# Two layers of a hybrid backbone on one core: the mixer in another order, attention's projections through DRAM, one attention routine

## The chip, the cores and the metric

The kernel runs on one core of a Trainium2 chip. The metric is the device time of one execution in microseconds. TensorE is called PE here (its weight loads, which overlap it, PEld), VectorE is DVE, ScalarE is ACT, GpSimd is POOL; SP is the queue that issues the DMAs.

## The reference, cut to what matters

Input is a latent stream x of 512 tokens and a context of 256 tokens, each 1024 wide. There are two layers. A layer is a feed-forward (half step), a mixer, and another feed-forward (half step):

```python
h, hc = modulate(rms_norm(x, g1), ..), modulate(rms_norm(xc, g1), ..)
p = h @ w_in[l]; pc = hc @ w_in[l]              # 3456 columns, cut into the groups' inputs
out_a = window_attn(rope(qa), rope(ka), va, ctx keys, sink)     # 4 heads of 64, window 128
out_b = global_attn(rope(norm(qb)), all keys, all values)       # 4 heads
out_c = retention, forward and backward, * silu(gates)          # 4 heads, chunks of 128
out_d = RWKV-7 recurrence, forward and backward, * (sigmoid(gd) @ g2)
x  = x  + mod[5]   * concat(out_a, out_b, out_c, out_d) @ w_out[l]
xc = xc + mod_c[5] * (the same for the context)                 # layer 0 only
```

The context sees only itself, and its mixer output is needed in layer 0 alone. So in layer 1 the queries, the gates and the outputs are made for 512 tokens, the keys and values for 768.

## The kernel before, in words

Activations lie transposed: a tile holds 128 features on the partitions and the tokens along the free dimension. The stream is eight such tiles, xT (128x768), which stay in SBUF through the whole program. Large products with a weight (feed-forward and `proj`, L926) run in three fp32r passes: weight and activation are each split in a high and a low part (`split`, L371: ACT makes the high part, DVE the rest), and `mm3` (L361) adds high*high, high*low, low*high. The split activations hh and hlo are made by the last step of the feed-forward. All other products are plain fp32, and each of those appears in the trace as two MATMULs.

`proj` loads one block of 128 columns of w_in (1024x128, 512 KB), splits it, runs 24 steps of `mm3` into two PSUM banks, and DVE (L945) and ACT (L946) bring the result to SBUF. A layer has 27 such blocks: ten for retention (C), eight for the attentions (A and B: k, v and two q tiles each) and nine for the recurrence (p0 to p8). A projection for all 768 tokens is called wide here, one for 512 tokens (layer 1's queries, gates, p0, p1, p6) half.

`mixer` (L1283) emits, in this order:

1. `group_c` twice: ten projections and retention.
2. `proj_ab` twice: eight projections, rotary, head norms, values turned to tokens on partitions.
3. `attend` (L1003): attention A, one unit for each head and block of 128 queries. A unit is scores (64 rows of the PE) into one PSUM tile of two banks (pool pS, one buffer), maximum (DVE), exp (ACT), a pass on DVE that divides by the sum, transposes, copies, and the product with V.
4. The nine projections p7, p8, p2, p3, p4, p5, p0, p1, p6; after p8 `rw_low`, after p3 `rw_lengths`.
5. The recurrence `rw_scan` (L844) over six blocks of 128 tokens in stages: decay (d), operands (o), inverse (i), late (l), steps (s), norm and output (y). All of attention B (`attend2`) is emitted between the first decay and the first operands. B's keys are padded with zeros to 128 rows, and its P*V takes two query blocks at a time; division by the sum comes at the end.
6. `out_proj` with A and C (64 fp32 products in layer 0), as a filler, then `out_proj` with B and D.

The Tile framework orders each engine's instructions when the program is built: emission order is the priority, and what is emitted later fills an engine when what is earlier isn't ready by the framework's own estimate. So step 3 runs among the projections of step 4, and step 6's first half among the steps of the recurrence. On the chip each engine takes its instructions in that fixed order and waits on semaphores. SP issues all DMAs, also in one fixed order.

The only state from one block of the recurrence to the next is S in `rw_step` (L770). `rw_inverse` (L705) is a chain of 30 small DVE operations (L725, L727) between transposes, ACT copies and four PE round trips; its start can be read from the one large transpose into Bu (L716), one for each block.

Of the kernel before, what the change touches and what calls it, by code (L numbers as in the profile page):

```python
# [113 lines left out]
class Whole:  # L114
    def __init__(self, ctx, tc, aps):
        self.tc, self.nc, self.a = tc, tc.nc, aps
        self.banks = {}
        self.macc = None
        self.const = self.pool(ctx, "const", 1)
        self.xp = self.pool(ctx, "xp", 1)  # L120
        self.work = self.pool(ctx, "work", 2)

    def psum(self, name, tag):
        pool, n = self.banks[tag]
        return pool.tile([128, 512], F32, name=name, tag=tag, bufs=n)

    def setup(self):
# [5 lines left out]
        self.xT = [self.xp.tile([128, T], F32, name=f"xT{k}") for k in range(KT)]  # L133
# [154 lines left out]
    def halves(self):  # L288
        t = self.pS.tile([128, 2, 512], F32, name="rst", tag="S")
        return [t[:, 0, :], t[:, 1, :]]  # L290

# [43 lines left out]
    def ready(self, l, n):  # L335

        def cb(k):
# [3 lines left out]
            self.raw_tile(k)  # L341
        return cb

# [116 lines left out]
    def rw_cols(self, l):  # L460
# [43 lines left out]
        self.rw2 = self.mp.tile([128, 2, 256], F32, name=f"rw2{l}")  # L504
# [29 lines left out]
    def rw_open(self, ctx):  # L534
        self.rp = self.pool(ctx, "rp", 1)
# [19 lines left out]
    def rw_lengths(self, p):  # L555
# [3 lines left out]
        for j in range(2):  # L559
            for d in range(2):  # L560
                z = self.ring("zkk")
# [282 lines left out]
    def rw_scan(self, p, bon, ctx_out, first):  # L844

        S = None
        N = T // 128
        has_r = lambda u: u > 1 or ctx_out
        st = [None] * (N + 2)
        Y = None  # L850

        def stage(k, u):
            nonlocal S, Y
# [11 lines left out]
            if k == "s":  # L865
                Y = self.rt.tile([128, NCH, 128], F32, name="Y", tag="Y", bufs=1) if h else None
                for c in range(NCH // 2):
                    S = self.rw_step(st[u], c, S, Y, h, u == 0 and c == 0)
            if k == "y" and h:
                self.rw_norm(Y)  # L870
                self.rw_out(Y, u, bon)

        stage("d", 0)
        for _ in first:
            pass
        for k, u in (("o", 0), ("d", 1), ("i", 0), ("l", 0)):
            stage(k, u)
        for u in range(N):
            for k, i in (("o", 1), ("s", 0), ("i", 1), ("d", 2), ("l", 1), ("y", 0)):
                stage(k, u + i)  # L880
# [43 lines left out]
    def proj(self, l, cols, both, evac):  # L924

        nc = self.nc  # L926
        r = self.praw.tile([128, KT, 128], F32, name="pw", tag="pw")
        o = 0
        for c0, n in cols:
# [587 lines left out]
```

## Time and profile before

| | |
|---|---|
| median of 3 runs | 3537.83 us (3533.33 to 3539.41) |
| the profiled execution | 3531.58 us, of it span 3529.8 us |
| granted PE clock, mean | 0.982 |
| busy of the span | PE 96%, PEld 78%, DVE 57%, ACT 32%, POOL 5% |
| chain that ended last | PE 84%, DVE 10%, ACT 3% |
| HBM read, written | 260.68 MB, 2.10 MB |

A busy PE is not PE at its peak: a matmul's record runs from its start to the end of its pipeline, so records overlap, and the distance of two starts in a dense row is what a matmul takes. The mixer of layer 0 lies at about 634 to 1340 us of the span, that of layer 1 at 2512 to 3112 us.

### The profile page before, as it was taken

The numbers are of one execution on the slowest core, as the hardware profiler recorded it, in microseconds if no ns is written. First come the engines' busy times: TensorE is split into PE (matmuls) and PEld (weight loads), VectorE is DVE, ScalarE is ACT, GpSimd is POOL, SyncE is SP. The second block draws the span as 40 slices with busy tenths as digits, with TensorE's granted clock in tenths as the row PEclk, the third lists the DMA queues.
The fourth block names the chain that finished last, engine by engine and source line by source line (L and its number), as shares of the span: only waits on it lengthen the run. The fifth ranks groups of instructions, "written<-read, shape, count | busy, mean of one in ns | idle before, by whom it ended". The sixth has DMA issues, their size and how long they took to land.

```text
span 3529.8 us, 54945 instructions
## 1 busy us (share of the span) xinstructions
PE 3372.1 (96%) x22756; PEld 2738.7 (78%) x22756; DVE 2002.2 (57%) x4351; ACT 1145.6 (32%) x2173; POOL 166.6 (5%) x350
## 2 busy tenths in 40 slices
PE   6999999999988899999999999999999988989997
PEld 5888888878666667888888788888878766557776
DVE  5776664555567856654335765543556577653333
ACT  3211122323456633121213221221324477432222
POOL 0000000000022400000000000000000023100000
PEclk9999999999999999999999999999999989999999
DMA  7444331211100014332222443330211100143230
GB/s 235 126 133 130 108 115 40 59 37 49 31 6 2 8 36 141 114 99 79 62 60 66 126 132 120 91 109 27 75 43 50 35 1 5 28 124 102 89 103 24
DMA packets 324122, 266.33 MB, mean 75 GB/s; under 512 B 27396, under 2 KB 273312, under 8 KB 323872
## 3 DMA queue, kind: packets, MB, share of 16 engines
q1 hardware_dynamic: 323872, 262.82, 24.4%
q8 instruction: 179, 2.93, 0.3%
q14 instruction: 71, 0.58, 0.1%
HBM read 260.68 MB, written 2.10 MB: 74 GB/s over the span
## 4 chain that ended last, share of the span: by engine, by line
PE 84%; DVE 10%; ACT 3%; DMA 1%; issue 1%; POOL 1%; SPq 0%; DVEq 0%; ACTq 0%; POOLq 0%
PE ul L365 13%; PE ul L369 13%; PE ul L367 13%; PE y L369 6%; PE y L367 6%; PE y L365 6%; PE pj L365 4%; PE pj L367 4%; PE pj L369 4%; PE op L1276 3%; PE S L1018 1%; PE ch L782 1%; DVE xtmp L725 1%; DVE w1l L378 1%; PE po L1018 1%
## 5 line engine op out<-in xcount | busy, mean ns | idle before, releaser
L365 PE MATMUL ul<-hh,w1h 128*128 128x512 f32 (+1 forms) x2464 | 693.5, 350 | 6.4 <-ACT w1h L377 5.6
L367 PE MATMUL ul<-hl,w1h 128*128 128x512 f32 (+1 forms) x2464 | 693.1, 348 | 0.0
L369 PE MATMUL ul<-hh,w1l 128*128 128x512 f32 (+1 forms) x2464 | 688.8, 348 | 2.2 <-DVE w1l L378 2.2
L365 PEld LDWEIGHTS ul<-hh,w1h 128*128 128x128 f32 x2464 | 395.9, 190 | 80.3 <-issue 9.9
L367 PEld LDWEIGHTS ul<-hl,w1h 128*128 128x128 f32 x2464 | 396.9, 190 | 64.1 <-issue 0.8
L369 PEld LDWEIGHTS ul<-hh,w1l 128*128 128x128 f32 x2464 | 393.7, 189 | 65.3 <-DVE w1l L378 3.7
L367 PE MATMUL y<-gl,w2h 128*128 128x512 f32 x1232 | 343.0, 347 | 4.3 <-DVE gl L431 4.0
L369 PE MATMUL y<-gh,w2l 128*128 128x512 f32 x1232 | 339.4, 346 | 5.8 <-DVE w2l L378 5.8
L365 PE MATMUL y<-gh,w2h 128*128 128x512 f32 (+1 forms) x1232 | 340.2, 347 | 1.1 <-ACT gh L430 0.9
L377 ACT ACTIVATE w1h<-w1r 128x2048 fp32r<-128x2048 f32 x88 | 168.7, 1917 | 479.6 <-PE ul L367 451.6
L215 DVE SCALAR_TENSOR_TENSOR macc<-wm,sc,macc 128x512 f32<-128x512 f32 x392 | 274.7, 749 | 78.8 <-DMA wm<-in_w_mod_dram 77.5
L445 DVE SCALAR_TENSOR_TENSOR xT<-y,gate,xT 128x512 f32<-128x512 f32 x336 | 199.3, 633 | 192.7 <-PE y L369 192.3
L377 ACT ACTIVATE w2h<-wo 128x512 fp32r<-128x512 f32 (+1 forms) x192 | 111.5, 594 | 547.0 <-PE y L367 351.8
L365 PE MATMUL pj<-hh,pwh 128*128 128x512 f32 (+2 forms) x864 | 251.8, 343 | 3.9 <-DVE qA L945 1.8
L369 PE MATMUL pj<-hh,pwl 128*128 128x512 f32 (+2 forms) x864 | 243.1, 336 | 2.4 <-DVE pwl L378 2.4
L367 PE MATMUL pj<-hl,pwh 128*128 128x512 f32 (+2 forms) x864 | 244.0, 337 | 0.0
L419 DVE TENSOR_TENSOR u<-ul,rsb 128x512 f32<-128x512 f32 (+1 forms) x132 | 70.9, 553 | 302.5 <-PE ul L369 302.5
L369 PEld LDWEIGHTS y<-gh,w2l 128*128 128x128 f32 x1232 | 195.0, 188 | 39.8 <-DVE w2l L378 10.0
L367 PEld LDWEIGHTS y<-gl,w2h 128*128 128x128 f32 x1232 | 195.4, 188 | 38.2 <-DVE gl L431 8.8
L365 PEld LDWEIGHTS y<-gh,w2h 128*128 128x128 f32 x1232 | 195.7, 188 | 37.6 <-ACT w2h L377 3.1
L378 DVE TENSOR_TENSOR w1l<-w1r,w1h 128x2048 fp32r<-128x2048 f32 x88 | 201.4, 2289 | 28.3 <-ACT w1h L377 28.3
L421 ACT ACTIVATE sg<-sg,ub 128x512 f32<-128x512 f32 (+1 forms) x132 | 74.2, 609 | 424.4 <-DVE ub L416 319.9
(355 smaller groups left out, 4495.9 us busy)
## 6 DMA issues: line engine op xcount, KB each, us to landing
w1r<-in_ffn_w_in_dram SPq DMA_DIRECT2D x176, 512.0 KB
wm<-in_w_mod_dram SPq DMA_DIRECT2D x72, 1024.0 KB
wo<-in_ffn_w_out_dram SPq DMA_DIRECT2D x88, 512.0 KB
pw<-in_w_in_dram SPq DMA_DIRECT2D x46, 512.0 KB
pw<-in_w_in_dram SPq DMA_DIRECT2D x16, 256.0 KB
wo<-in_w_out_dram SPq DMA_DIRECT2D x128, 32.0 KB
wo<-in_w_out_dram SPq DMA_DIRECT2D x64, 64.0 KB
xl<-in_x_dram SPq DMA_DIRECT2D x4, 512.0 KB
```

The costliest lines, as they stand in the source:

```text
L215: nc.vector.scalar_tensor_tensor(out=acc[v], in0=r[:, k, :], scalar=s, in1=acc[v], op0=ALU.mult, op1=ALU.add)
L365: nc.tensor.matmul(p, lhsT=wh, rhs=xh[:, o:o + n], start=first, stop=False)
L367: nc.tensor.matmul(p, lhsT=wh, rhs=xl[:, o:o + n], start=False, stop=False)
L369: nc.tensor.matmul(p, lhsT=wl, rhs=xh[:, o:o + n], start=False, stop=last)
L377: nc.scalar.activation(out=hi, in_=raw, func=AF.Copy)
L378: nc.vector.tensor_tensor(out=lo, in0=raw, in1=hi, op=ALU.subtract)
L419: nc.vector.tensor_tensor(out=dst[:, o:o + n], in0=p, in1=self.rsb[:, o:o + n], op=ALU.mult)
L421: nc.scalar.activation(out=dst[:, o:o + n], in_=dst[:, o:o + n], func=AF.Silu, bias=b[:, u, s:s + 1])
L445: nc.vector.scalar_tensor_tensor(out=xs, in0=py[s], scalar=gt[s][:, n_:n_ + 1], in1=xs, op0=ALU.mult, op1=ALU.add)
L725: nc.vector.tensor_tensor(out=tmp[:, :, :, :n], in0=Xv[:, :, :, s:16], in1=Bv[:, :, s:16, s].unsqueeze(2).to_broadcast([128, 2, 4, n]), op ...
L1018: mm = lambda out, lt, r, st, sp: nc.tensor.matmul(out, lhsT=lt, rhs=r, start=st, stop=sp, skip_group_check=True)
L1276: nc.tensor.matmul(p, lhsT=w[i], rhs=os[i][:, osegs[i][v][0]:osegs[i][v][0] + c], start=i == 0, stop=i == m - 1)
```

## The change

Order of the new mixer: retention with its ten projections; p7, p8, p2, p3, then p0, p1, p4, p5; the recurrence, with p6 and the eight attention projections emitted behind all its stages; then a second phase with both attentions and both output projections.

- The pool of xT is closed when the mixer begins. `put_away` writes each finished tile to DRAM in the last step of the feed-forward, and the tiles are read back for the output projections. Retention's two results and the eight attention inputs go to DRAM (`leave`) and are read back (`fetch`) in the second phase.
- A projection loads and splits its weight in two halves of 256 KB. For p6 and the attention inputs the load, the split and the way out of PSUM have a raised priority, the matmuls have not.
- One routine `attend` serves A and B: scores on 64 rows for both, two score buffers of two banks each, one bank (`ptr`) for the transposes, one query block at a time, division by the sum at the end (as B before).
- hh and hlo stay allocated. Retention has banks of its own (ms 2, ra 2, ro 1).
- `out_proj` takes C and D first, then A and B.

```diff
     def mixer(self, l, last_cb):
...
+        self.xx.close()
+        self.pd = {}
...
+    def scan_phase(self, sx, l, ctx_out, segs, bon, bons):
...
+            for j in range(2):
+                self.group_c(l, j, ctx_out)
...
+            for i in (7, 8):
+                proj(i)
+            self.rw_low(p[7], p[8])
+            for i in (2, 3):
+                proj(i)
+            self.rw_lengths(p)
...
+        stage = self.rw_scan(p, bon, ctx_out)
+        stage("d", 0)
+        for i in (0, 1, 4, 5):
+            proj(i)
+        for k, u in (("o", 0), ("d", 1), ("i", 0), ("l", 0)):
+            stage(k, u)
+        for u in range(T // 128):
+            for k, i in (("o", 1), ("s", 0), ("i", 1), ("d", 2), ("l", 1), ("y", 0)):
+                stage(k, u + i)
+        proj(6, True)
+        for g in range(2):
+            for name, cols, both in self.cols_ab(g):
+                self.proj_away(l, name, cols, ctx_out or both)
+        self.rw_gate(l, p[6], segs)
+        for j in range(2):
+            self.rw_final(l, j, bons[j], p[6], segs)
...
+    def heads_phase(self, tx, l, ctx_out, segs, gate, bons, last_cb):
+        self.psum_open(tx, pj=2, ptr=1, po=1)
+        self.alias = {"ms": "pj"}
+        self.pS = self.pool(tx, "pS", 2, space=PSUM)
...
+            for g in range(2):
+                self.prep_ab(g, ctx_out, *ab[g])     # fetch, head norms, rotary, V
+            self.wop = self.pool(px, "wop", 3)
+            for g in range(2):
+                for _ in self.attend(g, *ab[g], ctx_out):
                     pass
+            self.xT = [self.x_tile(k, "xT") for k in range(KT)]
+            for j in range(2):
+                self.fetch(f"oc{j}", oc[j])
+            for k in range(KT):
+                nc.sync.dma_start(out=self.xT[k][:, :n1], in_=self.away[k])
...
+            self.out_proj(l, [[(512 + 128 * i, 128)] for i in range(4)], oc + bons, ...)
+            self.out_proj(l, rows(0) + rows(1), ab[0][1] + ab[1][1], ..., last_cb)
...
     def proj(self, l, cols, both, evac, soon=False):
+        near = self.tc.high_priority if soon else ExitStack
+        H = KT // 2
+        for h in range(2):
+            with near():
+                r = self.praw.tile([128, H, 128], F32, name="pw", tag="pw")
...
+                wh, wl = self.split(r, [128, H, 128], "pw", self.phl)
+            for k in range(H):
+                self.mm3(...)
+    def proj_away(self, l, name, cols, both):
+        s = self.stg.tile([128, 771], F32, name="stg", tag="stg", bufs=2)
+        self.proj(l, cols, both, self.to_tile(s), soon=True)
+        with self.tc.high_priority():
+            self.leave(l, name, s, T if both else SEQ)
```

## Rows read from the trace of the kernel before

**Rows 1.** Six stretches of the mixers: us, busy (count) of each engine, PEclk, DMA

```profile
634.00:857.00 223.00, 218.94 (x1323) 175.29 (x1322) 110.89 (x263) 64.13 (x103) 2.45 (x28) 1.00 0.20 53
857.00:1018.00 161.00, 158.11 (x934) 119.37 (x934) 88.16 (x274) 74.35 (x172) 6.25 (x11) 0.98 0.09 26
1018.00:1301.00 283.00, 249.82 (x3408) 179.15 (x3407) 213.87 (x685) 172.31 (x477) 80.05 (x143) 0.97 0.04 11
2512.00:2695.00 183.00, 179.51 (x1212) 151.39 (x1211) 97.03 (x245) 57.05 (x97) 2.48 (x28) 1.00 0.24 64
2695.00:2828.00 133.00, 131.63 (x858) 104.08 (x858) 76.78 (x232) 65.81 (x140) 5.26 (x10) 1.00 0.11 32
2828.00:3085.00 257.00, 225.52 (x3139) 160.39 (x3138) 190.72 (x600) 162.74 (x442) 67.06 (x120) 0.92 0.04 11
```

**Rows 2.** Timeline of PE, a wide projection, then a half one: start, us, what

```profile
658.53 0.51 PE L365 MATMUL pj<-hh,pwh 128*128 128x512 f32 x2
658.88 0.52 PE L367 MATMUL pj<-hl,pwh 128*128 128x512 f32 x2
...
2692.18 0.40 PE L365 MATMUL pj<-hh,pwh 128*128 128x256 f32 x2
2692.42 0.41 PE L367 MATMUL pj<-hl,pwh 128*128 128x256 f32 x2
```

**Rows 3.** Line L946, both mixers: duration min/median/max, first to last start

```profile
L946 ACT ACTIVATE p<-p,pb x18: 494/608/726, 871.0 to 1018.5; 128x512 f32<-128x512 f32 x9, 128x256 f32<-128x256 f32 x9
L946 ACT ACTIVATE p<-p,pb x18: 492/506/727, 2709.5 to 2828.4; 128x256 f32<-128x256 f32 x12, 128x512 f32<-128x512 f32 x6
```

**Rows 4.** Line L716, layer 0 and its last three blocks, layer 1 likewise

```profile
L716 DVE STREAM_TRANSPOSE Bu<-Bc x6: 1242/1245/1246, 1048.1 to 1241.5; 128x1024 f32<-128x1024 f32 x6
L716 DVE STREAM_TRANSPOSE Bu<-Bc x3: 1245/1245/1246, 1175.4 to 1241.5; 128x1024 f32<-128x1024 f32 x3
L716 DVE STREAM_TRANSPOSE Bu<-Bc x6: 1234/1245/1246, 2852.5 to 3039.8; 128x1024 f32<-128x1024 f32 x6
L716 DVE STREAM_TRANSPOSE Bu<-Bc x3: 1245/1245/1245, 2967.3 to 3039.8; 128x1024 f32<-128x1024 f32 x3
```

**Rows 5.** Exponentials of attention A, layer 0, layer 1: duration, first to last start

```profile
L1037 ACT ACTIVATE P<-S,st x24: 475/689/808, 881.9 to 984.1; 128x512 f32<-128x512 f32 x8, 128x640 f32<-128x640 f32 x8, 128x256 f32<-128x256 f32 x8
L1037 ACT ACTIVATE P<-S,st x16: 673/740/797, 2719.0 to 2794.5; 128x512 f32<-128x512 f32 x8, 128x640 f32<-128x640 f32 x8
```

**Rows 6.** Two groups in 857 to 1018: busy us, mean ns, idle before

```profile
L567 PE MATMUL kkss<-mean,zkk 128*128 128x2 f32 x48 | 5.7, 246 | 0.0
...
L378 DVE TENSOR_TENSOR pwl<-pw,pwh 128x1024 fp32r<-128x1024 f32 x8 | 9.8, 1219 | 0.0
```

**Rows 7.** Timeline, weight loads of one unit of attention A [idle before, releaser]

```profile
943.84 0.73 PEld L1018 LDWEIGHTS S<-kv,qA 64*128 64x128 f32 x4 [0.25 <-ACT st L1038]
945.11 0.42 PEld L1048 LDWEIGHTS ptr<-ident,P 128*128 128x128 f32 x4 [0.54 <-issue]
946.57 0.85 PEld L1018 LDWEIGHTS po<-PT,kv 128*64 128x64 f32 x14 [0.26 <-ACT PT L1049]
```

**Rows 8.** Timeline of PE, output projections of layer 0, end of layer 1's

```profile
1334.82 1.88 PE L1276 MATMUL op<-qB,wo 128*128 128x512 f32 x4
1336.54 1.88 PE L1276 MATMUL op<-kv,wo 128*128 128x512 f32 x4
...
3110.57 1.88 PE L1276 MATMUL op<-kv,wo 128*128 128x512 f32 x4
```

**Rows 9.** Timeline of PE, retention's scores of one head and of two

```profile
782.81 0.49 PE L1221 MATMUL ra<-q,k 64*128 64x128 f32 x2
...
784.17 0.49 PE L1221 MATMUL ra<-q,k 64*128 64x128 f32 x4
```

**Rows 10.** Two weight loads issued after layer 0's mixer, and the first matmul behind

```profile
1339.31 1.00 SPq L393 DMA_DIRECT2D w1r<-in_ffn_w_in_dram  x2
...
1347.33 1.01 PE L365 MATMUL ul<-hh,w1h 128*128 128x512 f32 x2 [1.49 <-ACT w1h L377]
```

More of the change, by code (lines that the diff above doesn't have):

```diff
@@ L865, in stage @@
             if k == "s":
-                Y = self.rt.tile([128, NCH, 128], F32, name="Y", tag="Y", bufs=1) if h else None
-                for c in range(NCH // 2):
-                    S = self.rw_step(st[u], c, S, Y, h, u == 0 and c == 0)
+                c[1] = self.rt.tile([128, NCH, 128], F32, name="Y", tag="Y", bufs=1) if h else None
+                for i in range(NCH // 2):
+                    c[0] = self.rw_step(st[u], i, c[0], c[1], h, u == 0 and i == 0)
             if k == "y" and h:
[L870 to L880, printed above, removed]
+                self.rw_norm(c[1])
+                self.rw_out(c[1], u, bon)
+        return stage
     def pool(self, ctx, name, bufs, **k):
@@ L922, in first_mods, with proj @@
             self.raw_shifts(0, 0)
-    def proj(self, l, cols, both, evac):
+    def proj(self, l, cols, both, evac, soon=False):
         nc = self.nc
-        r = self.praw.tile([128, KT, 128], F32, name="pw", tag="pw")
-        o = 0
-        for c0, n in cols:
-            nc.sync.dma_start(out=r[:, :, o:o + n], in_=self.a["w_in"][l, :, c0:c0 + n].rearrange("(k p) n -> p k n", p=128))
-            o += n
-        wh, wl = self.split(r, [128, KT, 128], "pw", self.phl)
+        near = self.tc.high_priority if soon else ExitStack
@@ new lines, in proj_away, with leave, fetch @@
+    def proj_away(self, l, name, cols, both):
[3 more added lines that the diff above has]
+            self.leave(l, name, s, T if both else SEQ)
+    def leave(self, l, name, s, n):
+        t = self.dram.tile([128, n], F32, name=f"{name}d{l}")
+        self.nc.sync.dma_start(out=t, in_=s[:, :n])
+        self.pd[name] = t, n
+    def fetch(self, name, t):
+        d, n = self.pd[name]
+        self.nc.sync.dma_start(out=t[:, :n], in_=d)
+        return t
@@ L1001, in tokens_major, with attend @@
             nc.scalar.copy(V[:, b0:b0 + nb, :], pt[:, :nb * 128].rearrange("p (b n) -> p b n", n=128))
-    def attend(self, ab, ctx_out):
-        nc = self.nc
-        kT, qs, V = ab[0][0], ab[1:3], ab[3].rearrange("p (b n) -> p b n", n=128)
+    def attend(self, g, kT, qs, V, ctx_out):
+        nc, ap = self.nc, self.ap
+        mm = lambda out, lt, r, st, sp: nc.tensor.matmul(out, lhsT=lt, rhs=r, start=st, stop=sp, skip_group_check=True)
+        hs = [(hf, slice(64 * hf, 64 * hf + 64)) for hf in range(2)]
@@ L1216, in group_c @@
                 hs = [(e, slice(64 * e, 64 * e + 64)) for e in range(2)]
-                pts = [self.psum("ra", tag) for tag in ("ptr", "ms")]
+                pts = [self.psum("ra", "ra") for e in range(2)]
                 for e, r in hs:
@@ L1236, in group_c @@
                                 nc.tensor.matmul(ws(r, d), lhsT=state[d][b][r], rhs=qw[d][r, cs], start=False, stop=True, skip_group_check=True)
-            for d in range(2):
-                nc.scalar.copy(od[d][:, o_:o_ + n], po[:, d, :n])
+                for d in range(2):
+                    nc.scalar.copy(od[d][:, cs], po[:, d * 128:(d + 1) * 128])
         for d in range(2):
@@ L1361, in rope_tab @@
-    def rope_tab(self, c0, r0):
+        self.xx.close()
+        self.pd = {}
+        with ExitStack() as mx:
+            self.bp = self.pool(mx, "bp", 1, side="right")
+            bon = self.bp.tile([128, 2, T], F32, name="bon")
+            bons = [bon[:, j, :] for j in range(2)]
+            with ExitStack() as sx:
+                self.scan_phase(sx, l, ctx_out, segs, bon, bons)
+            with ExitStack() as tx:
+                self.heads_phase(tx, l, ctx_out, segs, gate, bons, last_cb)
+            self.alias = {}
```

452 lines of the change are left out of this document (190 added, 262 removed).

## The prediction

> **What bounds the kernel now.** I read the busy shares first (the table above): PE is busy in 96% of the span, so only stretches where its work is thin have something to give. The busy time by stretch finds them, once each mixer is cut at places where the code changes over: the end of the first eighteen projections, of the last projection, of the recurrence with the first output projection [rows 1]. Up to 857 us (layer 0) PE is busy in 219 of 223 us. From 857 to 1018, nine projections with attention A between them, in 158 of 161. From 1018 to 1301, recurrence, attention B and first output projection, in 250 of 283, while DVE is busy in 214. Layer 1 shows the same, its last stretch at a granted clock of 0.92.
>
> The timeline tells what PE's work should take. A wide projection is 24 steps of 0.35 us, 8.45 us, a half one 24 of 0.24, 5.7 us [rows 2]. An fp32 product with 512 columns takes two passes of 0.43, 0.86 us [rows 8]. So nine projections in layer 0 are 76 us, and 857 to 1018 leaves 85 for attention A and smaller work.
>
> The recurrence is read from the start of its inverse, once a block. The first comes 29.6 us after the last projection's evacuation in layer 0 (1018.5 to 1048.1), 24.1 in layer 1 [rows 3, 4]. Over all six blocks the distance is 38.7 and 37.5 us, over the last two, behind attention B, 33.0 and 36.2 [rows 4]. The recurrence is thus a chain bound by DVE and round trips, and attention B on the same engines stretches it.
>
> **The change part by part.** The sum follows one mixer at a time from its first eighteen projections to the last output projection.
>
> *First eighteen projections.* Eight blocks of the recurrence stand where eight of attention stood. In layer 0 all are wide: end at 857 as now. In layer 1 six wide and two half replace four and four: 2 x (8.45 - 5.7) = 5.5 us later, 2701. The split in halves leaves PE's work alone; the weights in hand cover 4.2 us instead of 8.4. Where DVE or ACT is held longer than that PE waits: 0 to 8 us a layer, against which retention gets more banks (0 to 8 gained). I take 0, since PE's share in [rows 1] leaves 4 us in 223 to move. The writes of xT are 8 DMAs a layer behind feed-forward matmuls; nothing waits for them but pools that retention doesn't need first. If SP holds a weight load behind one, the nearest price is the load of [rows 10], 8 us from issue to first matmul, so 0 to 8; I take 0.
>
> *Start of the recurrence.* It needs p2 and p3 (through at 857 - 34 = 823), the key lengths, decay and operands; p4 and p5 come later. The lengths are 48 small matmuls (5.7 us [rows 6]) with as much ACT and DVE, some 15 us, decay and operands some 20 (of the 29.6 above): first inverse at 860 in layer 0 and likewise 2706 in layer 1. Upper end: 857 + 29.6 = 887, and 2701 + 24 = 2725.
>
> *The recurrence.* Five distances. With attention B gone from DVE and ACT I take 34 us, near layer 0's last ones (33.0); upper end 38.7 [rows 4]. What fills PE now is nine projections, 76 and 62 us, which need no softmax between matmuls; they bring some 2.5 us each to DVE at raised priority (the split 1.22 [rows 6], the way out of PSUM about as much), in the place of the output projection's evacuations. Each leaves for DRAM through one of two staging tiles; its DMA waits on SP for the evacuation, and behind it stand only the next weight halves, which PE needs 4 us later. From the last inverse to the end of the recurrence is 1301 - 1241.5 = 59 us in layer 0 with output projection mixed in, 3085 - 3039.8 = 45 in layer 1 [rows 1, 4]; I take 46, whose cover is layer 1's. End: 860 + 170 + 46 = 1076, and 2706 + 170 + 46 = 2922.
>
> *Second phase.* First its attention. Of 161 us in layer 0, 76 are projections and some 17 smaller groups (kkss 5.7 [rows 6], head norms, rotary and first decay by like counts); 68 remain for A's 24 units (16 latent, 8 context). In layer 1 133 - 68 (six wide, three half) - 9 = 56 for 16 latent units: 3.5 us each, so 1.5 a context unit. The starts of their exponentials lie 102/23 = 4.4 and 76/15 = 5.0 us apart, projections included [rows 5]. B's latent units have 768 scores where A's mean is 576: 192 x 2 x 0.43/512 = 0.32 us, and 1.5 more transposes and products 0.32: 4.1 us. Two score buffers and no dividing pass on DVE between exp and transposes take, by my choice, 0.2 from each: 3.3 and 3.9. Layer 0: 16 x 3.3 + 16 x 3.9 + 16 x 1.5 = 139. Layer 1: 16 x 7.2 = 115. The first output projection can only lie between these: 8 x 4 x 0.86 = 27.5 us, and 41 with the context [rows 8].
>
> Then its start, which had projections as a cover and now has none. The fetched tiles overlay the recurrence's last, so they wait for its end, and on SP all loads of the phase stand behind the first of them; fetch and first rotary some 10 us (two loads of 512 KB took 8 with their split [rows 10]), then norms, rotary and transposes on PE, 15 and 12 us. Sum: 139 + 41 + 25 = 205, and 115 + 27.5 + 22 = 165. Lower end: every unit at its pure columns, 0.43 us for 512 a pass (two passes of scores, one of transposes, half of two for V: A 1.9, B 2.6, context 0.9), 153 and 122. Upper end: latent units at 5.0 us [rows 5], 250 and 210.
>
> *Last output projection.* As now: 39 and 27 us; 8 DMAs a step instead of 6, which PE's 5.2 and 3.4 us a step cover.
>
> *Sum.* Layer 0: 1076 + 205 + 39 = 1320 where 1340 was, -20. Layer 1: 2922 + 165 + 27 = 3114 where 3112.4 was, +2. Together -18 on the profiled execution's own 3531.6: 3513.6. The median shown is 6.2 above that execution: 3520.
>
> A's unit costs more than its columns because PE pauses where its work changes: 0.25 us before the scores, 0.54 before the transposes, 0.26 before the product with V [rows 7]. A's 3.5 us, from which B's is made, has these pauses in it, so the sum holds none besides; if B's move from 128 rows to 64 adds two more of 0.25 to each of its 32 latent units, that is 16 us. The Trainium skill, TensorEngine Tiling (Array Packing), section Key Properties, says that a change of tiling mode drains the array. It speaks against this change: by it the sum would be 3536 and not 3520; the pauses in the trace fit it, though those rows don't tell a drain from a wait.
>
> **The rivals.**
>
> *The second phase is faster.* Two score buffers let the scores of both heads of a pair stand next to each other, on different rows. Retention's scores show it: four passes of two heads take 0.49 us, as two passes of one do [rows 9]. Against it: buffers come free one at a time. With half of the scores' time gone (layer 0 16 x 0.97 + 16 x 1.29 + 16 x 0.43 = 43, layer 1 36; half of both 40) 3480; with 0.5 us of pauses hidden in each of 64 latent units too, 3450. The same skill page, Tiling Modes, allows 64-row tiles to run in parallel, a gain of up to two.
>
> *The second phase is slower (the other side).* One bank takes every transpose; a unit needs PE, ACT copy, PE, DVE copy in turn on it, and now only output projection fills. Above 3.6 + 18/64 = 3.9 us a latent unit the gain is gone. At 5.0 us it is +45 in each layer: 3610.
>
> *The recurrence isn't relieved.* Raised splits and evacuations take attention's place on DVE; distances stay at 38.7: 10 x 4.7 = 47, 3567. For it: DVE is busy in 214 of 283 us. Against: nine projections bring 22 us of DVE to a whole layer, under 4 a block.
>
> *Nothing in the sum.* What the first part gains (219 us hold recurrence and nine projections) the second phase takes: it stands 18 us from that, and the two more pauses a unit of B's [rows 7] end here too (3536). 3531 to 3545.
>
> **How the numbers follow.** The forecast (3493 to 3531) 38%, the faster second phase 15%, nothing 16%, the slower second phase 21%, the unrelieved recurrence 10%. A change within 0.2% (7 us) can't be told from none. So faster 0.53, same 0.16, slower 0.31. Steps can add: low end 3452 (the faster rival with a little of the recurrence at 33), high end 3590 (most of the slower one). The forecast's own range is 3493 to 3531.
>
> **What would show each step.** Inverse starts: first within 10 us of the eighteenth projection, then 33 to 36 apart; at 38 the recurrence isn't relieved. From its end to the first score some 10 us of idle PE. Exponentials of latent units 3.6 us apart on average: 3.0 is the faster rival, 4.5 the slower. The second phase up to the last output projection 205 and 165 us. The prediction is wrong if the recurrence with nine projections takes over 240 us, if retention's stretch grows by more than 10, or if SP shows weight loads waiting behind the writes of xT.

## The result, and the profile after

The changed kernel takes 3567.41 us (median of 4 runs, 3566.36 to 3580.15), the one before in the same session 3537.62: a ratio of 1.0094, interval 1.007 to 1.0119. It is slower by 30 us by the medians, by 33 by the ratio, where 3520 was predicted. The profiled execution took 3566.67 us, of it span 3564.9; its mean granted clock is 0.973 (before 0.982), PE is busy in 96% as before, and the chain that ended last is 84% PE, 8% DVE, 4% ACT, 2% DMA.

The stretches of [rows 1], as they lie now: first eighteen projections, recurrence with nine projections, second phase, last output projection, for each layer (us, then busy us and count of PE, PEld, DVE, ACT and POOL, then PEclk, the share and the GB/s of DMA).

```profile
632.50:868.00 235.50, 230.77 (x1390) 187.26 (x1389) 131.90 (x368) 95.48 (x201) 12.37 (x52) 0.98 0.18 54
868.00:1112.00 244.00, 220.47 (x3320) 179.07 (x3318) 179.47 (x576) 148.75 (x377) 74.34 (x129) 0.98 0.13 38
1112.00:1311.00 199.00, 192.76 (x1104) 116.05 (x1104) 89.53 (x277) 75.29 (x186) 0.00 (x0) 0.95 0.13 45
1311.00:1354.00 43.00, 41.94 (x132) 24.55 (x130) 24.27 (x38) 14.48 (x22) 0.00 (x0) 1.00 0.15 40
2521.00:2717.00 196.00, 193.57 (x1290) 164.56 (x1289) 118.63 (x350) 88.69 (x193) 4.81 (x40) 0.98 0.21 63
2717.00:2947.00 230.00, 203.51 (x3181) 171.48 (x3179) 161.83 (x525) 140.86 (x360) 69.16 (x117) 0.91 0.12 36
2947.00:3114.00 167.00, 161.29 (x867) 96.00 (x867) 72.02 (x208) 57.39 (x126) 0.00 (x0) 0.87 0.15 47
3114.00:3151.00 37.00, 32.65 (x64) 9.89 (x62) 10.53 (x15) 4.41 (x7) 0.00 (x0) 1.00 0.18 49
```

From the start of the last product of the feed-forward before a mixer to the first of the one behind it, layer 0 takes 728.1 us (before 713.0) and layer 1 638.4 (611.7); the feed-forwards are together some 7 us shorter. So the loss is in both mixers. The inverse starts, which answer [rows 4] (duration, first to last start), and the exponentials of the second phase, which answer [rows 5]:

```profile
L733 DVE STREAM_TRANSPOSE Bu<-Bc x6: 1245/1245/1246, 873.9 to 1058.5; 128x1024 f32<-128x1024 f32 x6
L733 DVE STREAM_TRANSPOSE Bu<-Bc x6: 1245/1246/1246, 2721.8 to 2896.0; 128x1024 f32<-128x1024 f32 x6
...
L1065 ACT ACTIVATE P<-S,st x48: 462/744/906, 1128.9 to 1293.7; 128x256 f32<-128x256 f32 x16, 128x768 f32<-128x768 f32 x16, 128x512 f32<-128x512 f32 x8, 128x640 f32<-128x640 f32 x8
L1065 ACT ACTIVATE P<-S,st x32: 669/850/907, 2963.5 to 3096.8; 128x768 f32<-128x768 f32 x16, 128x512 f32<-128x512 f32 x8, 128x640 f32<-128x640 f32 x8
```

The five distances are 36.9 us on average in layer 0 and 34.8 in layer 1; the recurrence ends 53.6 and 51.1 us after its last inverse starts. Its end is here and below the end of its last product, `gd`: at 1293.3 and 3085.8 us in the kernel before, at 1112.1 and 2947.0 now.

```profile
1111.43 0.70 PE L1423 MATMUL gd<-p,g 128*128 128x256 f32 x2 [0.84 <-DVE bon L1424]
```

| step, us | predicted, layer 0 / 1 | measured |
|---|---|---|
| mixer's start to the 18th projection | 223 / 189 | 235 / 195 |
| to the first inverse | 3 / 5 | 6 / 5 |
| five distances | 170 / 170 | 185 / 174 |
| last inverse to the recurrence's end | 46 / 46 | 54 / 51 |
| second phase up to the last output projection | 205 / 165 | 199 / 167 |
| last output projection | 39 / 27 | 41 / 36 |

By this table the two mixers are 60 us over the sum: the recurrence (distances and end) 32, the first eighteen projections 18, the last output projection 11, the start of the recurrence 3, the second phase 4 under. The shorter feed-forwards take 7 of it back, and 53 is what lies between 3513.6 and the profiled 3566.7.

### The profile page after: what moved, and what is told of

It reads as the page before. It is cut to its first block, busy times and chain, and to the rows that moved or that the text cites. A ratio compares the mean times of both kernels' runs of the same rounds, so it can differ in the third digit from the quotient of the medians.

```text
span 3564.9 us, 55890 instructions
## 1 busy us (share of the span) xinstructions
PE 3413.6 (96%) x23044; PEld 2761.4 (77%) x23044; DVE 1977.2 (55%) x4351; ACT 1156.1 (32%) x2187; POOL 169.6 (5%) x358
## 4 chain that ended last, share of the span: by engine, by line
PE 84%; DVE 8%; ACT 4%; DMA 2%; issue 1%; POOL 1%; SPq 0%; DVEq 0%; ACTq 0%; POOLq 0%
PE ul L383 12%; PE ul L385 12%; PE ul L387 12%; PE y L387 6%; PE y L385 6%; PE y L383 6%; PE op L1235 4%; PE S L1032 3%; PE pj L383 3%; PE pj L385 3%; PE pj L387 3%; PE ch L799 2%; PE po L1032 2%; PE ptr L1077 2%; PE gram L670 1%
## 5 line engine op out<-in xcount | busy, mean ns | idle before, releaser
L383 PE MATMUL pj<-hh,pwh 128*128 128x512 f32 (+2 forms) x864 | 243.4, 343 | 5.2 <-DVE p L957 3.9
```

What stands on the lines that cost most here:

```text
L383: nc.tensor.matmul(p, lhsT=wh, rhs=xh[:, o:o + n], start=first, stop=False)
```

## The experiments

Each stands with its edit, the expectation on record, and the reading; `...` marks lines left out of an edit. "Length of the recurrence" is from the first inverse to its end, layer 0 / layer 1: 245 / 233 us before, 238 / 225 changed, 216 / 216 predicted.

**1. Most matmuls of the nine projections left out (e1_nomm).**

```diff
-            for k in range(H):
+            for k in (range(H) if not soon else [(H - 1) * h]):
                 self.mm3(outs, wh[:, k, :], ...)
```

> Leaves out 18 of the 24 steps of every projection emitted behind the recurrence (p6 and the eight attention inputs); their loads, splits, evacuations and DRAM writes stay. Theory A, PE is shared: in the profile of the changed kernel the recurrence's stretch of layer 0 (868 to 1112 us) has PE busy 220 of 244 us, of which 76 are the nine projections, so the chain's matmuls queue behind them. Then the distance of two inverse starts falls from 36.9 us (layer 0) and 34.9 (layer 1) to 29 to 32, and the recurrence ends some 35 us earlier in layer 0 and 20 in layer 1. Theory B, the chain of DVE, ACT and round trips sets the distance: 35 to 37 us stay, and the time falls by under 10 us in all. Between them: 33 us, about what was predicted, would say that half of the excess comes from PE.

3613.6 us: 46 slower with less work. The length was 260 / 238, the distances 40.8 and 37.2. Theory A's shorter distances didn't come. But the granted clock fell as well, to 0.76 from 0.97 (875 to 1060 us in layer 0), so the run doesn't say that PE's work is no limit at the full clock.

**2. The nine projections left out wholly (e2_nofill).**

```diff
-        proj(6, True)
...
-                self.proj_away(l, name, cols, ctx_out or both)
+        nc.gpsimd.memset(p[6], 0.5)
...
+                s = self.stg.tile([128, 771], F32, name="stg", tag="stg", bufs=2)
+                nc.gpsimd.memset(s, 0.5)
+                self.leave(l, name, s, ...)
```

> Leaves out the same nine projections wholly (no loads, no splits, no evacuation; GpSimd fills the tiles, which are written to DRAM as before). Theory A: as with most of their matmuls left out, the distance stays within 1 us of that run's. Theory C, the raised splits and evacuations on DVE and ACT (some 2.5 us on DVE a projection, 22 us a layer) stretch the chain: the distance is 3 to 4 us shorter than with only the matmuls left out, and most of the excess over 34 goes here and not there.

3587.0 us (ratio 1.0149): slower than with them. The length was 247 / 226. The windows from the 18th projection to the recurrence's end:

```profile
873.00:1126.00 253.00, 180.52 (x2897) 150.78 (x2895) 163.64 (x532) 128.55 (x339) 73.94 (x129) 0.68 0.03 8
2741.00:2971.00 230.00, 162.59 (x2747) 137.91 (x2746) 144.15 (x481) 122.14 (x323) 63.54 (x117) 0.71 0.03 7
```

The reader is to see the clock column: 0.68 and 0.71 against 0.98 and 0.91 with the projections. PE was busy in 71% of either stretch, TensorE spent more than half of it at 1.2 GHz, and the recurrence's own products, which stand on the chain one behind the other, took longer: in layer 0 those of `gram` 409 ns on average for 303, those of `ch` 266 for 229. Neither A nor C is told by these two runs, since the clock changed with what was left out.

**3. The same number of matmuls with nothing else (e5_pefill).**

```diff
-        proj(6, True)
...
-                self.proj_away(l, name, cols, ctx_out or both)
+                for k in range(KT):
+                    self.mm3(outs, self.hh[:, k, :128], self.hlo[:, k, :128], self.hh[:, k], self.hlo[:, k], segs2, ...)
...
```

> Leaves out what the nine projections behind the recurrence do outside PE (loads, splits, evacuation; GpSimd fills their tiles) but keeps the same number of three-pass matmuls of the same shapes, from tiles that are in place, with nothing waiting for them. With no projections at all (e2_nofill) the distance of inverse starts was 38.3 us in layer 0 and 35.3 in layer 1 at a granted clock of 0.70 in 875 to 1060 us; with all of them 36.9 and 34.8 at 0.97. Theory C, at the full clock it is the splits and evacuations on DVE and ACT that keep the distance up: 33 to 34 in layer 0 and 32 in layer 1, some 15 us a layer earlier at the recurrence's end. Theory B, the chain has its own length: 36 to 37 and 34 to 35, as with everything. Theory A, PE's queue: the same as B here, but then the run with no matmuls, which differs in the clock alone, cannot tell them apart.

The windows from the 18th projection to the recurrence's end:

```profile
870.00:1119.00 249.00, 223.01 (x3322) 183.46 (x3320) 161.40 (x530) 128.01 (x340) 73.16 (x129) 0.95 0.03 10
2730.00:2956.00 226.00, 204.60 (x3183) 171.90 (x3182) 144.84 (x480) 122.76 (x324) 65.41 (x117) 0.92 0.04 11
```

3571.6 us. Distances fell to 35.0 and 32.9, as theory C wants, but the time from the last inverse to the end grew to 68.8 and 57.4: length 244 / 222. So what the splits and evacuations held up in one place was found again at the end; PE had the same work (223 us busy against 220) and gave the same stretch or a little more, 249 against 244 and 226 against 230.

This run is run 2 with matmuls of no use put in, and it is 15 us faster than run 2 (by the medians of two runs each; the intervals, 1.0078 to 1.0131 and 1.0131 to 1.0168, just meet). With the clock at 0.95 and 0.92 for 0.68 and 0.71 the stretches are 249 for 253 and 226 for 230 us. So part of what the left-out work cost there came by the clock.

**4. No raised priority (e8_no_raise).**

```diff
-        near = self.tc.high_priority if soon else ExitStack
+        near = ExitStack
...
-        with self.tc.high_priority():
+        with ExitStack():
             self.leave(l, name, s, T if both else SEQ)
```

> The nine projections behind the recurrence without the raised priority of loads, splits, evacuation and DRAM writes. Theory C: what is raised delays the chain on DVE and ACT (22 us a layer); without it distances fall to 34 and the recurrence ends 5 to 15 us earlier in each layer, 3540 to 3558. Rival: weights now come late, PE starves and projections are left over at the recurrence's end: 3570 to 3600. No effect: 3563 to 3570.

3565.1 us, ratio 1.009 (1.007 to 1.011), no effect on the time: length 243 / 228, distances shorter (35.6, 34.6), the end later, as in the run before. Theory C is out: without the raise, or without the splits and evacuations themselves (run 3), the stretch from the 18th projection on takes 249 us in layer 0 for 244, and 232 and 226 in layer 1 for 230.

**5. GpSimd's clearing moved (e6_uv_late).**

```diff
-            nc.gpsimd.memset(UV[hu:hu + 64], 0.0)        # in rw_ops, ahead of the other direction's zr and AR
+        for hu, x in zip((0, 64), st):                   # in rw_late
+            nc.gpsimd.memset(x["UV"][hu:hu + 64], 0.0)
```

> The recurrence's clearing of UV on GpSimd (first thing in a block's operand stage) is moved to its late stage, behind the same block's zr, AR and zv. In the changed kernel GpSimd waits for PE ahead of it 49.8 us in two blocks (940 to 1022 us, idle 50 of 82), because UV has two buffers and the block before the last one has to be through its steps; zr and AR of the new block stand behind it in GpSimd's queue, and the operands need them. Theory D: this wait sets the distance of 40 us in layer 0's middle blocks: distances 34 to 36 in both layers, 10 to 25 us less in all, 3543 to 3557. Rival B: GpSimd has time to spare (70 of 185 us busy) and other links set the distance: no change, 3563 to 3570.

3565.1 us, ratio 1.0085 (1.0067 to 1.0103): nothing. The waits of GpSimd, 940 to 1022 us (waited for: us, times, longest):

```profile
POOL UV L688 <- PE ch L800: 50.5, 2, 28.6
```

The wait is still there at its new place, 50.5 us for 49.8, and the distances are the same (37.0 and 34.6). It was spare time, not a link: a long wait is only worth removing if somebody waits for the waiter. Theory D is out.

**6. A shorter chain (e10_short_inverse).**

```diff
-        for s in range(14, -1, -1):
+        for s in range(2, -1, -1):
```

> The changed kernel with 3 of the 15 steps of the inverse's loop of small DVE operations (24 of 30 operations left out; the recurrence's outputs then mean nothing). By the rows a pair takes 0.31 + 0.22 us, so DVE is relieved of 6.4 us a block. Theory B1, the inverse is a link of the loop from block to block: the distance falls by 5 to 7 us (36.9 to 31, 34.8 to 29) and the time by 50 to 70 us. Theory B2, the loop closes over other links (operands, GpSimd, steps, norm) and the inverse runs beside them: the distance falls by 0 to 2 us.

The windows of the same two stretches, then of what lies behind the last inverse's start:

```profile
870.00:1099.00 229.00, 216.13 (x3322) 177.14 (x3320) 154.19 (x433) 147.68 (x377) 70.50 (x129) 1.00 0.14 41
2710.00:2925.00 215.00, 200.24 (x3181) 169.47 (x3179) 138.71 (x381) 140.66 (x360) 61.95 (x117) 0.95 0.14 41
...
1016.50:1099.00 82.50, 78.40 (x824) 63.66 (x820) 35.05 (x98) 28.14 (x58) 1.15 (x8) 1.00 0.30 90
2859.00:2925.00 66.00, 63.78 (x802) 54.95 (x796) 31.56 (x92) 26.68 (x56) 1.57 (x9) 1.00 0.34 100
```

3530.0 us, 37 less, where 50 to 70 were expected. Distances fell to 28.1 and 28.8, so the inverse is a link of the loop (B1), but of the 38 us of DVE that a layer lost, the stretch from the 18th projection to the recurrence's end shrank by only 15 in each. What was left behind the last inverse is bound by PE: busy in 78 of 82 and 64 of 66 us, at the full clock. The last of the nine projections is evacuated 4.3 and 2.0 us before the end; in the changed kernel that is 4.3 us in layer 0, but 30 in layer 1, where PE has only the recurrence's own products left (19 of 30 us busy, clock 0.59):

```profile
2917.00:2947.00 30.00, 19.38 (x260) 14.22 (x254) 8.34 (x28) 5.93 (x16) 1.08 (x7) 0.59 0.16 51
```

The recurrence has two limits close to each other: its chain, and the sum of PE's work in it. In layer 0 PE's work reaches to the end; in layer 1 the end is the chain's.

**7. Attention B left out of the kernel before (e9_before_no_b).**

```diff
-                self.rw_scan(p, bon, ctx_out, self.attend2(ab[1], ctx_out))
+                self.rw_scan(p, bon, ctx_out, ())
```

> The kernel before with attention B left out (its units between the first decay and the first operands of the recurrence are not emitted; the output projection takes B's queries as they are). All else stays, the first output projection among the recurrence too. From the first inverse to the end of the recurrence the kernel before takes 245 us in layer 0 and 233 in layer 1; the changed one 238 and 225; with no projections behind it at all 247 and 226. Theory B, the recurrence has its own length, which the work beside it hardly moves: 235 to 248 and 225 to 235 here as well, and the whole gets 15 to 60 us faster at most, from what B pushed out of it. The prediction's reading, attention B stretches it: some 216 us (five distances of 34 and 46) in each layer.

3467.2 us, ratio 0.9811: 66 us less. The length was 228 / 215, so B did stretch the recurrence, by 17 and 18 us; layer 1 came out as the prediction read it, though at a lower clock than with B (rows below; before 0.97 and 0.92):

```profile
1016.00:1265.00 249.00, 201.62 (x3056) 152.23 (x3054) 183.75 (x581) 139.22 (x377) 83.57 (x143) 0.87 0.05 12
2791.00:3026.00 235.00, 184.29 (x2852) 138.49 (x2851) 162.67 (x518) 134.59 (x360) 67.88 (x120) 0.82 0.05 13
```

That 66 is all that B's 40 units cost there, 1.7 us each.

**8. Attention B left out of the changed kernel (e13_after_no_b).**

```diff
-            for g in range(2):
+            for g in range(1):
                 for _ in self.attend(g, *ab[g], ctx_out):
```

> The changed kernel with attention B's units left out of the second phase (its projections, fetch, head norms and rotary stay). Theory, B is exposed here: the second phase has PE busy in 193 of 199 us, so B's 32 latent and 8 context units are worth their PE time, 32 x 3.9 + 8 x 1.5 = 137 us: 3425 to 3445. In the kernel before the same units were worth 66 us (e9_before_no_b). Rival, the waits of A and of the fetch grow when B no longer fills them: 3480 to 3500, a price as before.

3448.4 us, ratio 0.976 where the changed kernel has 1.0094: 0.0334 x 3535 = 118 us, near the 137 of its units' PE time and far from 66. What is left of the second phase:

```profile
1116.00:1255.00 139.00, 133.34 (x641) 81.86 (x642) 57.89 (x186) 41.63 (x110) 0.00 (x0) 0.88 0.19 63
2883.00:2994.00 111.00, 105.42 (x480) 62.06 (x481) 45.30 (x141) 31.54 (x76) 0.00 (x0) 0.81 0.22 69
```

139 and 111 us instead of 199 and 167, 116 together, with PE full in both. B is exposed there.

**9. First output projection left out, before and changed (e14_before_no_op1, e16_after_no_op1).**

```diff
 # before
-                for _ in fill:
-                    pass
 # changed
-            self.out_proj(l, [[(512 + 128 * i, 128)] for i in range(4)], oc + bons, ...)
```

> The kernel before with its first output projection (A and C, among the recurrence's steps) left out. Theory, it was hidden in the recurrence: its 41 and 27.5 us of PE columns are worth 10 to 35 us in all, 3498 to 3523. Rival, PE's total was the bound there (busy 220 of 245 us): 50 to 69 us, 3465 to 3485.

> The changed kernel with its first output projection (C and D) left out. Theory, exposed: the second phase is full, so it is worth its 41 and 27.5 us of columns, 55 to 69 us, 3498 to 3512. Rival, it only filled waits of the attention units: 10 to 40 us, 3527 to 3557.

Before: 3532.9 us, ratio 0.9994 (0.9979 to 1.0009), worth nothing, less than either side of the expectation. Changed: 3547.5 us, ratio 1.0032 (1.0005 to 1.006), worth some 22 us, in the range of the rival, with wide limits (both intervals together give 4 to 40). The stretch of the kernel before without it, and layer 0's with it (layer 1's is in [rows 1]):

```profile
1017.00:1297.00 280.00, 225.78 (x3279) 173.18 (x3278) 207.78 (x668) 171.75 (x477) 80.14 (x142) 0.86 0.02 5
2820.00:3077.00 257.00, 204.59 (x3067) 157.28 (x3067) 185.81 (x591) 161.70 (x441) 64.83 (x117) 0.85 0.02 5
...
1018.00:1293.00 275.00, 241.82 (x3385) 174.74 (x3384) 212.20 (x682) 172.31 (x477) 80.05 (x143) 0.97 0.04 10
```

280 and 257 us where 275 and 257 were with it, at a clock of 0.86 and 0.85 instead of 0.97 and 0.92. Its products are busy some 43 and 35 us in these stretches, yet PE's busy time is only 16 and 21 us more with them. That its work cost nothing because it kept the clock up fits these rows; no run holds the clock without it, so it isn't shown.

**10. Nine projections left out of the kernel before (e15_before_no_nine).**

```diff
-                    self.proj(l, [(2304 + 128 * i, 128)], ...)
+                    for o, n in ((1, 256), (258, 512)):
+                        self.nc.gpsimd.memset(p[i][:, o:o + n], 0.5)
```

> The kernel before with the recurrence's nine projections left out (GpSimd fills their tiles). Theory, they are exposed there (PE busy 158 of 161 us): 76 and 62 us of columns, 110 to 138 us, 3395 to 3425. Rival, attention A's units among them were covered by them and now wait: 70 to 100 us, 3435 to 3465.

3555.8 us, 21 slower without them. Attention A's stretch, first to last exponential, without the projections and with them (before, same stretch):

```profile
883.00:1005.00 122.00, 102.94 (x377) 61.03 (x377) 45.86 (x128) 35.64 (x102) 2.41 (x4) 0.54 0.00 1
2731.00:2827.00 96.00, 82.26 (x300) 50.66 (x301) 33.54 (x85) 26.67 (x71) 2.25 (x4) 0.54 0.00 1
```

```profile
882.00:984.00 102.00, 101.92 (x601) 71.40 (x602) 57.31 (x155) 48.30 (x123) 2.54 (x4) 1.00 0.09 27
2719.00:2794.00 75.00, 74.82 (x452) 52.39 (x452) 43.28 (x107) 37.11 (x88) 2.19 (x4) 1.00 0.10 29
```

Alone A takes 122 and 96 us at a clock of 0.54; with projections among it 102 and 75 at 1.00. Both theories fell. In the kernel before the projections fit among attention A's units without lengthening them, and with them the clock there is 1.00.

**11. Fewer DMAs for the output weights (e3_dma).** The last output projection of layer 1 in the changed kernel, PE and then SP's queue, which answer the end of [rows 8]:

```profile
3113.78 9.94 PE L1235 MATMUL op<-q,wo 128*128 128x512 f32 x22
3123.87 1.10 PE L1235 MATMUL op<-q,wo 128*128 128x512 f32 x2 [0.16 <-DMA wo<-in_w_out_dram]
3125.27 1.10 PE L1235 MATMUL op<-q,wo 128*128 128x512 f32 x2 [0.30 <-DMA wo<-in_w_out_dram]
```

```profile
3008.02 139.82 SPq L1230 DMA_DIRECT2D wo<-in_w_out_dram  x84
```

```diff
-            for i, runs in enumerate(ks):
-                for r0, cnt in runs:
-                    nc.sync.dma_start(out=wt[p:p + cnt, i, :], in_=a["w_out"][l, r0:r0 + cnt, ...])
+            for dst, r0, cnt in ks:      # one of 4 x 128 rows; or four of 2 x 64 rows
+                nc.sync.dma_start(out=dst(wt), in_=a["w_out"][l, r0:r0 + cnt, ...].rearrange("(i p) n -> p i n", ...))
...
```

> The output projections load their weights with fewer DMAs: 1 a step instead of 4 for the first, 4 instead of 8 for the second (two column tiles in one DMA of 64 rows). In layer 1 of the changed kernel the second one takes 36.5 us for eight steps, and its weight loads wait for DMAs on SP that are 0.66 us apart, 5.3 us for eight. Theory: SP's issue is the bound; layer 1's second output projection falls to 28 us, layer 0's (43 us, 5.2 us of PE a step) by 0 to 2; 3567 becomes 3556 to 3559. Rival: the bytes or the landing of 64-row pieces is the bound, not the issue: no change, 3565 to 3569.

The same place of PE's timeline in this run:

```profile
3115.31 27.63 PE L1232 MATMUL op<-q,wo 128*128 128x512 f32 x64
```

Shown: the 64 products of layer 1 stand in one dense row of 27.6 us instead of 36, without a wait. In all 3562.9 us, ratio 1.0079 (1.0066 to 1.0091), 5 less by the medians, inside the two intervals.

**12. Scores of two heads next to each other (e4_pairs).**

```diff
+                    ss = [self.pS.tile([128, 1024], F32, name="S", tag="S") for _ in hs]
+                    for hf, rows in hs:
+                        with self.tc.high_priority(offset=hf):
+                            mm(ss[hf][:, 256:512], qh[hf], kT[rows, SEQ:T], True, True)
```

> In the attention routine the scores of both heads of a block are emitted next to each other (one head on rows 0 to 63, the other on 64 to 127), each into its own score buffer. The changed kernel's 160 score matmuls of layer 0's second phase take 60 us of PE. Theory: on different rows two run at once, as retention's scores do (four passes of two heads 0.49 us, two of one head 0.49): 20 to 30 us less in layer 0 and 15 to 25 in layer 1, 3515 to 3535. Rival: both score buffers are now held by one block until its exponentials are through, PE waits for ACT, and the gain is given back: 3560 to 3580.

Four passes of 256 columns that are neighbours on PE's timeline, of two heads in this run and, below it, of one head in the changed kernel:

```profile
1181.90 0.80 PE L1032 MATMUL S<-kT,q 64*128 64x256 f32 x4
```

```profile
1150.89 1.13 PE L1032 MATMUL S<-kT,q 64*128 64x256 f32 x4
```

Four passes of two heads take 0.80 us, four passes one behind the other 1.13. But few came to stand so (53 of the 288 passes start within 0.1 us of the one before, 7 in the changed kernel), and the time was 3564.5 us, ratio 1.0081 (1.0066 to 1.0096): no difference.

**13. Both heads in one PSUM tile; B's preparation later (e11_one_tile_pairs, e12_and_prep_late).** Both have the DMAs of run 11 and the order of run 12; the edit is shown against run 12. The second run also emits `prep_ab(1, ...)` behind attention A.

```diff
-                    ss = [self.pS.tile([128, 1024], ...) for _ in hs]
+                    s2 = self.pS.tile([128, 2, 1024], F32, name="S", tag="S")    # pool of one buffer
+                    ss = [s2[:, hf, :] for hf in range(2)]
...
```

> The weights of the output projections by fewer DMAs (as in e3_dma, -5 us), and the scores of both heads of a block in one PSUM tile of four banks instead of two tiles of two, so that both heads' scores become ready together. With two tiles (e4_pairs) only 53 of 194 neighbouring score matmuls started within 0.1 us of each other, since the second buffer came free later; PE's time in scores fell from 56 to 52 us in layer 0 and from 50 to 41 in layer 1. Theory: nearly all pair now, 30 us of scores in layer 0 and 26 in layer 1, some 40 us less, 3520 to 3535. Rival: with one buffer a block's scores wait for both exponentials of the block before, and PE idles 1 to 2 us in each of 40 blocks: 3560 to 3590.

> As e11_one_tile_pairs, and B's head norms, rotary and values are emitted behind attention A instead of before it, so that A's first scores don't stand behind them. In the changed kernel the first exponential comes 16.5 us after the recurrence's end. Theory: it comes 8 to 10 us after it, and B's preparation fills PE's waits in A: 5 to 15 us below e11_one_tile_pairs. Rival: PE is full in this phase, so the order of the same work changes nothing: within 4 us of it.

3571.2 us, ratio 1.01 (1.0083 to 1.0117), and with the later preparation 3561.2 us, 1.0078 (1.0057 to 1.0099). PE's waits in layer 0's second phase with one tile:

```profile
PE ptr L1085 <- ACT P L1073: 15.4, 16, 2.2
PE ptr L1085 <- ACT PT L1087: 4.7, 7, 0.7
```

Scores fell from 60 and 52 to 41 and 35 us of PE, and in layer 0 PE waits 20 us for ACT, where it waited 2.2 before: the rival. The later preparation is 10 us less by the medians, with intervals that overlap, but not by the step expected: the first exponential still came 14.5 and 14.4 us after the recurrence's end, where 8 to 10 were expected.

**14. Useless matmuls to hold the clock (e7_warm).**

```diff
+        for i in range(8 if ctx_out else 20):     # 8 matmuls each, behind the projections; 64 more in the second phase
+            nc.tensor.matmul(w[:, :256], lhsT=self.hh[:, k, :128], rhs=self.hh[:, k, :256], ...)
...
```

> Adds useless matmuls (256 columns, hh on hh) to the changed kernel: 64 in layer 0 and 160 in layer 1, emitted behind the projections, so that they fill the last part of the recurrence, and 64 (some 8 us) at the start of each second phase, while its tiles are fetched. In the changed kernel the granted clock is half (1.2 GHz) from 2918 to 2956 and 2959 to 2993 us in layer 1 and from 1113 to 1137 in layer 0, after PE's work had become thin. Theory E, the clock has a price there: layer 1 gets 10 to 20 us shorter in spite of the added work, 3548 to 3560. Rival: recurrence tail and fetch are bound by waits and not by PE, and the added work costs what it takes: 3567 to 3585.

3578.5 us, ratio 1.0119 (1.01 to 1.0138), 11 us slower by the medians. The clock did rise (mean 0.980), and layer 1's mixer took 634 us instead of 638, but layer 0's took 742 instead of 728: its projections already last to the end of the recurrence, and the added work came on top. Theory E wins in layer 1 by 4 us, where 10 to 20 were expected, and loses in layer 0 by 14. In layer 1 the second phase up to the last output projection took 160 us for 167, but the recurrence's end, from its last inverse, no less (changed kernel, then this run):

```profile
2896.00:2947.00 51.00, 38.54 (x621) 31.17 (x617) 25.77 (x94) 15.91 (x38) 1.08 (x7) 0.76 0.11 37
```

```profile
2912.00:2966.00 54.00, 52.21 (x795) 46.26 (x789) 25.79 (x94) 16.34 (x39) 1.09 (x7) 1.00 0.18 57
```

None of these versions that compute the whole reaches the kernel before.

## Why the prediction was wrong, step by step

**First eighteen projections: put too early, by 12 and 6 us.** The prediction counted only blocks of columns here. PE was full (231 of 235 us), so the small products that were moved ahead of the eighteenth projection came on top:

```profile
L584 PE MATMUL kkss<-mean,zkk 128*128 128x2 f32 x48 | 5.6, 247 | 0.0
L670 PE MATMUL gram<-AR,BK 128*128 128x128 f32 x16 | 1.9, 275 | 0.0
L612 PE MATMUL wa<-tw,rw 64*128 64x128 f32 x8 | 1.3, 297 | 0.0
L612 PE MATMUL wa<-ta,rw 64*128 64x128 f32 x8 | 1.2, 272 | 0.0
L302 PE MATMUL kkn<-ident,rb 128*128 128x128 f32 x8 | 1.2, 288 | 0.1
```

The key lengths (`kkss`) and the first block's are 11 us of busy PE in layer 0. The prediction's own sign, a growth of this stretch by more than 10 us, came true there. The prediction had the 5.7 us of [rows 6] in the step behind it, and there they took nothing: the first inverse followed by 6 and 5 us, where 3 and 5 were foreseen.

**The recurrence: this step failed.** It was put at five distances of 34 and an end of 46 us, 216 in all, with nine projections that "fill PE" and cost no time there; it took 238 and 225. PE's sum was never made: 220 us busy in layer 0's stretch, 76 of them the projections (144 are the recurrence's own), against 219 allowed for it. It took 244. Without B the kernel before came close to 216 (228 / 215), and with the nine projections in B's place the changed kernel is some 10 us above that in each layer (238 / 225).

The rival of an unrelieved recurrence had the right time (3567) by luck: its distances of 38.7 didn't come (36.9 and 34.8), and the raised splits and evacuations, its mechanism, are worth nothing (runs 3 and 4). The chain and PE's sum hold the recurrence together: with the chain shortened PE binds (run 6), with the projections gone the chain does, at a clock of 0.68 (run 2). That is layer 0's case. In layer 1 the projections are through 30 us before the end, so PE's sum doesn't explain the end there (51 us for 46), and the run that raised the clock there didn't shorten it (run 14); this part of the cause stays open, as does the link of the chain that makes the middle distances of layer 0 longest.

**The trade, which hung on it.** The prediction gave the change 161 us of projections and A, and 64 of the recurrence, in layer 0, against 205 for the second phase. The prices by leaving out tell what the pieces were worth (us, both layers):

| piece | in the kernel before | in the changed one |
|---|---|---|
| attention B | 66 | 118 |
| first output projection | 2 | 22 |
| nine projections | -21 | -19 |

B cost half of the 137 us of PE time put for it inside the recurrence and the first output projection nothing; behind it the two are 72 us dearer. The projections were already free, among attention A, and are free again, in another place; their prices are below zero because the clock falls without them. Against the 72 stands the start of the recurrence: from the projection it waits for to the first inverse 29.6 and 24.1 us before, 5.8 and 4.7 now, 43 us gained. These prices are differences of whole kernels, in which the clock moves too, and attention A was not priced; they fit the sign and the size (72 - 43 = 29), and aren't a full account of the 33.

**The second phase: right.** 199 and 167 us for 205 and 165. The 16 us that two more pauses a unit would have cost B in both layers together don't show in this sum; but it is made of estimates, and no run moves B back to 128 rows. So the rule of the Trainium skill in TensorEngine Tiling (Array Packing), Key Properties, that a change of tiling mode drains the array, is neither shown nor refuted here. The start came about as put: the first score is 11.2 and 11.8 us after the recurrence's end for "some 10", though PE isn't idle all that time but makes the rotary products, and the first exponential is 16.8 and 16.5 us after it:

```profile
1115.43 2.05 PE L991 MATMUL rot<-kT,axial 128*128 128x512 f32 x2 [3.15 <-issue]
...
1123.36 2.07 PE L1032 MATMUL S<-kT,q 64*128 64x256 f32 x4
```

The phase runs in part at 1.2 GHz (PEclk 0.95 and 0.87 in the two stretches), and the units were a little cheaper: in layer 1 (133.3 - 27.5) / 31 = 3.4 us for 3.6. The faster rival didn't come true by itself: the two heads' passes were not next to each other. Where they were (run 12) four passes took 0.80 us for 1.13. The Trainium skill, TensorEngine Tiling (Array Packing), Tiling Modes, lets 64-row tiles run in parallel, and these rows agree.

**The last output projection: mis-sized in layer 1.** "8 DMAs a step, which PE's 3.4 us cover": SP issues one every 0.64 us (5.1 us a step), and it took 36 us for 27. Run 11 shows the cause and gives 9 back in that place; of the whole time 5 us by the medians, inside the intervals.

## What to carry to other kernels

A stretch that is bound by a chain is a host: other work in it can cost less than its own time (here the first output projection nothing, B half), and can keep the clock up. So before work is moved out of one, price it there by leaving it out, not by its columns, and sum PE's own work of the host with the guest's before saying that the chain gets shorter. When a transfer is cut in pieces, count the pieces against the issue time of one, step by step.

## What the runs showed of the hardware that was not expected

- Work left out can cost time. Three kernels that leave out the nine projections or most of their matmuls got 19 to 46 us slower. In each the granted clock of the thinned stretch fell: to 0.76 with most matmuls gone, to 0.68 and 0.71 in the recurrence with all gone (layer 0: PE busy 181 of 253 us, idle at most 5.0 us at a time), to 0.54 in attention A alone (103 of 122, at most 1.5).
- Matmuls of no use bought time in one place and not in another. In place of the missing projections they gave 15 us back (run 3 against run 2); added to the changed kernel they raised the mean clock from 0.973 to 0.980 and cost 11 us (run 14).
- Half the bytes took SP longer: in layer 1's second phase the DMAs of 64 rows (32 KB), one behind the other, occupy it 0.595 us each, those of 128 rows (64 KB) 0.33 to 0.43.
